# Later rotary products and weight preparation, an earlier first norm, and rebalanced helpers in a one-core decoder step

## The chip, the core and the metric

The kernel runs on one NeuronCore of a Trainium2 chip. The metric is device time in microseconds (us) of one execution. TensorE (PE in the profile) does the matrix products, VectorE (DVE), ScalarE (ACT) and GpSimd (POOL) do everything else, and all DMAs are issued from SyncE's queue (SP).

## What is computed

One layer of a hybrid decoder, for 1024 prompt positions and 8 x 4 sample positions that share the weights: 1056 columns in all, held feature-major (features on the 128 partitions, positions along the free axis). Cut to what matters here:

```python
h   = rmsnorm(x)
q, k, v, g, su, sv, xq, gates = split(h @ w_in)
A   = retention(rope(q), rope(k), v)      # 4 heads, chunks of 128, then GroupNorm and silu(g)
B   = gelu(su) * (tril(W_s) @ layernorm(gelu(sv)) + b)   # per chunk of 128, 4 channel groups
C   = cross_attention(xq, memory)         # 4 heads, 256 memory tokens
x   = x + (sig(gA)*A@w_br_ret + sig(gB)*B@w_br_sg + sig(gC)*C@w_br_x) @ w_o
z   = rmsnorm(x) @ w_up                   # then causal depthwise conv of width 3
x   = x + (gelu(conv(z)[:F]) * conv(z)[F:]) @ w_down
y   = rmsnorm(x)
```

rope turns the halves of a head: `x1*cos - x2*sin` and `x2*cos + x1*sin`.

## The kernel before

**Products.** Every float32 operand is split into a high part in the matmul's reduced type (`hi = cast(x)`, on ACT) and a low part (`lo = x - hi`, on POOL or DVE), and a product is three matmuls: high x high, high x low, low x high. A projection `fm(key, ops)` runs eight steps, one for each 128 input features; a step is nine matmuls (three terms by three column chunks of 384, 384 and 288). `psv` gives its PSUM tile `mp`, of which there are two. Small products (norm sums, retention, attention) use `ap`, also two.

**Weights.** `w_prep` takes the next weight slab (128x1024) from its DMA, casts it (`wh`, ACT) and subtracts (`wl`). The subtraction is on POOL, except for the keys in the list `LO_DVE`, for which it is on DVE. `w_ahead` calls `w_prep` when fewer than three slabs are live; `fm` calls it at two of its steps, before the step's `hook`. So a slab is prepared some two projections before it is used.

**What sets the order.** The order of instructions on each engine is that of the Python code; there is no scheduler behind it. `hook`, called after each step, (1) counts down the list that `later(n, fn)` fills and runs what is due, (2) runs one entry of `side`, and (3) advances the generator at the head of `gens` by `rate[0]` steps on average. The generators carry the work that runs beside the projections: `xnorm` (the first norm), `retention` of the head before, `sgu`, `xattn`, `half_norm`, `last_conv`, `fin`.

**The places that the change touches.**

- Head 0: q and k are projected together (`fm2`, 16 steps), then two g units of 8 steps. `xnorm` yields `YA` times, squares the last four of the eight x tiles (`xr`, ACT), adds them up (DVE), yields `YB` = 3 times, casts the sum (`rsh`, `rsl`), multiplies it with ones on PE (`ap`), and forms the reciprocal root by a table and a Newton step. The V projection of head 0 waits for the PSUM of g, which is scaled by that root.
- `rope_evac`, after each q and k: the product with the cosines from PSUM (DVE), four copies of the swapped halves (`sw`, ACT), the product with the sines (`sw`, POOL), and later the sum (DVE). Reads of one PSUM tile by two engines are ordered as the code has them.
- `retention`: for each chunk, `norm_rows` takes statistics (DVE) and gets the reciprocal root `grs` from two tiny POOL instructions; then DVE scales the row, and C multiplies into `ort`, which frees an `ap`.
- `sgu`: eight rounds of four matmuls into an `ap`, an addition from PSUM (`sgt`) and a product (`su`) on DVE.
- `xattn(h)`: `QS` splits the head's query (`xqh` ACT, `xql` DVE), `KS` a half of the cached keys.
- `gate(key)`: after a projection, DVE scales (`th`), ACT takes the tanh, and a DMA stores it.
- w_o: two halves of 528 columns, eight units each; a unit's result is added to the residual (`x2c`, DVE), squared (ACT) and summed (DVE), while `half_norm` works on the first half.
- w_down: eleven pairs of weight rows; a pair is eight units of 18 matmuls, each added into `x` by DVE. `last_conv`, in five steps, runs the last convolution's taps (`c`, DVE) beside the first units.
- The end: the last two pairs in three column ranges (512, 288, 256); `fin(c)` makes the final norm of a finished range: the sum of squares `ssf` is split (`sy`), summed by PE, and eight products `y` follow on POOL. `fin_last` is the same for the last range, with nothing behind it.

Of the kernel before, what the change touches and what calls it, by code (L numbers as in the profile page):

```python
# [9 lines left out]
F32R = mybir.dt.float32r  # L10
AF = mybir.ActivationFunctionType
ALU = mybir.AluOpType
# [62 lines left out]
HA, HB = 248, 280  # L75

LO_DVE = [k for i, k in enumerate(SLABS) if k[0] in ("km", "vm") and i % 2] + [("sv", 0, 0), ("sv", 0, 1)]


@with_exitstack  # L80
def step_kernel(ctx: ExitStack, tc: tile.TileContext, xT, memT, wslab, cst, ident_d, rope, vec, sgc, sgm, sgs,
                sret, kc, vc, hist, yT, sretp, cstate, ckT, cv, srets, sgv):
    nc = tc.nc
# [8 lines left out]
    def slot(name, dt=F32, shape=None):  # L92
        return sp.tile(shape or [P, T], dt, tag="S", name=name, bufs=NSLOT)
# [13 lines left out]
    def mm(out, l, r, start=True, stop=True):  # L107
        nc.tensor.matmul(out=out, lhsT=l, rhs=r, start=start, stop=stop)  # L108
# [4 lines left out]
    def vtt(out, a, b, op):  # L113
        nc.vector.tensor_tensor(out=out, in0=a, in1=b, op=op)  # L114

    def ptt(out, a, b, op):
        nc.gpsimd.tensor_tensor(out=out, in0=a, in1=b, op=op)  # L117
# [4 lines left out]
    def f(t):  # L122
        return t.bitcast(F32) if t.dtype == F32R else t

    def psv(ps):
        return [ps[:, 0:2, 0:384], ps[:, 2, 0:288]]

    def seg(t):
        return [t[:, 0:768].rearrange("p (a b) -> p a b", a=2), t[:, 768:1056]]
# [58 lines left out]
    def later(n, fn):  # L188
        wait.append([n, fn])
# [41 lines left out]
    def fm(key, ops, kbase=0, free=True):  # L231
        hi, lo = w_get(key)
        hv = hi.rearrange("p (k c) -> p k c", c=P)
        lv = lo.rearrange("p (k c) -> p k c", c=P)
        ps = mp()
        n = len(ops)
        for k in range(n):
            rh, rl = ops[k]
            for i, (a, r) in enumerate(((hv, rh), (hv, rl), (lv, rh))):
                for c, (c0, w) in enumerate(CH):  # L240
                    mm(ps[:, c, 0:w], a[:, kbase + k, :], r[:, c0:c0 + w],
                       start=(k == 0 and i == 0), stop=(k == n - 1 and i == 2))
            if k == 0 or k == 3:
                w_ahead()
            hook()
        if free:
            w_free(key)
        return ps
# [107 lines left out]
    with tc.manual_schedule():  # L356
# [70 lines left out]
        nc.vector.tensor_scalar(out=vecs[:, VBG:VBG + 32], in0=vecs[:, VBG:VBG + 32], scalar1=0.5, scalar2=None,  # L427
                                op0=ALU.mult)

        YA, YB = 14, 3  # L430

        def xnorm():
            for _ in range(YA):
# [41 lines left out]
        def rope_evac(ps, name):  # L475
            sw = slot("sw")
            out = slot(name)
            for o, i, c in zip(seg(out), psv(ps), seg(cosT)):
                vtt(o, i, c, ALU.mult)
            for (a, b) in ((0, 64), (64, 0)):  # L480
                for o, i in zip(seg(sw), psv(ps)):
                    nc.scalar.copy(out=o[a:a + 64], in_=i[b:b + 64])
            ptt(sw, sw, sinT, ALU.mult)
            later(4, lambda: vtt(out, out, sw, ALU.add))
            return out

        def silu_evac(ps):
# [457 lines left out]
        def xattn(h):  # L945
# [133 lines left out]

            for fn, *a in ((XA, 0), (YA, 0), (XA, 1), (YA, 1), (XB, 0), (VS, 0), (XB, 1), (XC, 0), (VS, 1), (XA, 2), (YB,),  # L1080
                           (XC, 1), (XB, 2), (XA, 3), (YC, 0), (XC, 2), (KS, h + 1, 0), (XB, 3), (YC, 1),
                           (KS, h + 1, 1), (XC, 3), (QS, h + 1), (YD,)):
                while defer:
                    defer.pop(0)()
                fn(*a)
                if fn not in (VS, KS, QS):
                    yield
# [168 lines left out]
        def gate(key):  # L1256
            ps = fm(key, hops)
            t = slot("th")
            scaled(t, ps)
            return lambda: gate_out(t, key)  # L1260
# [38 lines left out]
        for m in range(8):  # L1299
            if m == 6:  # L1300
                side.extend([g_load] * 8)
            if m == 7:
                side.extend([lambda k=k: g_scale(k) for k in range(8)])
            gate(("gb", m))()
        drain()
        rate[0] = 0.0
        side.extend([lambda: f_dma(NG), lambda: G0s(0), both(G0s, 1), lambda: f_prep0(NG), both(G0s, 3), both(G0s, 5),
# [532 lines left out]
        pctx.close()  # L1840
        mpp = pctx.enter_context(tc.tile_pool(name="mpp2", bufs=2, space=bass.MemoryType.PSUM))
        gens.append(last_conv())
        rate[0] = 1.0

        def dn_get(g):
            ws = []
# [42 lines left out]

        ssf = slot("ssf")  # L1890
        rsy = slot("rsy")
        sy3 = slot("sy3", F32R)
        FCH = ((0, 512), (512, 288), (800, 256))

        def fin(c):
            c0, w = FCH[c]
            r = rsy[:, c0:c0 + w]
            yield
            yield from rstd_cols(ssf[:, c0:c0 + w], w, r, sy3, fine=True)
            for m in range(0, 8, 2):  # L1900
                y = slot("y", shape=[P, 2, 512])
                for i in range(2):
                    ptt(y[:, i, 0:w], x2t[m + i][:, c0:c0 + w], r, ALU.mult)
                later(2, lambda m=m, y=y: dma(yT[m:m + 2, :, c0:c0 + w].rearrange("m p t -> p m t"), y[:, :, 0:w]))
                yield

        def fin_last(sqs):

            c0, w = FCH[2]
            r = rsy[:, c0:c0 + w]  # L1910
            a = ap()[:, 0:w]
            mm(a, ones, sy3[:, 0:w], stop=False)
            mm(a, ones, sy3[:, w:2 * w], start=False, stop=False)
            for i in range(2):
                mm(a, f(ones), sqs[i], start=False, stop=(i == 1))
            t = slot("rn")
            rstd_sum(a, r, t[:, 0:w])
            x = lambda m: x2t[m][:, c0:c0 + w]
            g = lambda m: vecs[:, VFN + m:VFN + m + 1]
            for m in (3, 7):  # L1920
                act(x(m), x(m), scale=g(m))
            newton(r, t[:, 0:w], t[:, w:2 * w])
            for m in range(0, 8, 2):
                y = slot("y", shape=[P, 2, 512])
                for i in range(2):
                    if m + i in (3, 7):
                        ptt(y[:, i, 0:w], x(m + i), r, ALU.mult)
                    else:
                        stt(y[:, i, 0:w], x(m + i), g(m + i), r, ALU.mult, ALU.mult)
                dma(yT[m:m + 2, :, c0:c0 + w].rearrange("m p t -> p m t"), y[:, :, 0:w])  # L1930
# [5 lines left out]
        def fin_evac(c, us, pss):  # L1936
            c0, w = FCH[c]
            sl = slice(c0, c0 + w)
            sqs = {}
            for m in us:  # L1940
                vtt(x2t[m][:, sl], x2t[m][:, sl], pss[m], ALU.add)
            for m in us:
                sqs[m] = ssf[:, sl] if m == 0 else slot("sq")[:, 0:w]
                act(sqs[m], x2t[m][:, sl], AF.Square)
            for m in us:
                if c == 2 and m > 5:
                    last_sq.append(sqs[m])
                elif m:
                    vtt(ssf[:, sl], ssf[:, sl], sqs[m], ALU.add)
            if c == 2 and us[-1] == 5:  # L1950
                nc.scalar.copy(out=sy3[:, 0:w], in_=ssf[:, sl])
                vtt(sy3[:, w:2 * w], ssf[:, sl], f(sy3[:, 0:w]), ALU.subtract)
            for m in us:
                if c < 2:
                    act(x2t[m][:, sl], x2t[m][:, sl], scale=vecs[:, VFN + m:VFN + m + 1])
# [174 lines left out]
```

## Time and profile before

| | |
|---|---|
| time, median of 3 runs (lowest to highest) | 1917.12 us (1916.0 to 1917.32) |
| the profiled execution's time | 1916.06 us |
| its span from first to last instruction | 1913.9 us |
| mean granted TensorE clock | 0.991 |
| PE busy | 1854.7 us (97%) |
| DVE, POOL, ACT busy | 1144.7, 921.5, 651.8 us |
| HBM read, written | 154.34 MB, 48.41 MB |

PE is busy for nearly the whole span, so a change is worth what it takes from, or adds to, the 59 us in which PE does nothing and the time in which its clock is low. Times in the rows are us from the span's start: a row of the timeline gives start, duration, engine, line, operation, tiles (output <- inputs), count, and in brackets the idle time of the engine just before it with what ended it.

### The profile page before, as it was taken

To read this page: it belongs to the slowest core of one execution; us is meant where nothing else is said; L and a number is where in the kernel's file an instruction comes from. 1 tells how busy PE (TensorE), PEld (TensorE's weight loads), DVE (VectorE), ACT (ScalarE), POOL (GpSimd) and SP (SyncE) were. 2 spreads that over 40 slices of the span, in tenths; PEclk is the share of its full clock that TensorE was granted. 3 is DMA by queue.
4 is the path that set the end of the run, shared out by engine and by line. 5 is a ranking of instruction groups with operands and counts; after the bars stand their busy time and mean duration, and the time that the engine had idled before them with its cause. 6 is when DMAs were issued, how large, how long until landed. Compare 5 with 4: busy or idle time off the path is not lost.

```text
span 1913.9 us, 32100 instructions
## 1 busy us (share of the span) xinstructions
PE 1854.7 (97%) x13369; PEld 1828.0 (96%) x13369; DVE 1144.7 (60%) x1610; ACT 651.8 (34%) x1016; POOL 921.5 (48%) x583
## 2 busy tenths in 40 slices
PE   8899999999999999999999999899999999999997
PEld 8899999999999998999999999899999999999996
DVE  6554545442464479332352267999999999744447
ACT  6333232421233434323211233544344344321204
POOL 2243434221643421555544533577777777754404
PEclk9999999999999999999999999999999999999998
DMA  5112131324133341426632532022222223732202
GB/s 189 54 45 93 44 105 36 132 66 156 56 135 112 124 181 55 135 90 255 241 124 79 189 140 84 34 90 79 68 90 79 67 90 120 252 133 90 76 1 91
DMA packets 59808, 204.82 MB, mean 107 GB/s; under 512 B 6608, under 2 KB 9840, under 8 KB 59664
## 3 DMA queue, kind: packets, MB, share of 16 engines
q1 hardware_dynamic: 59664, 202.78, 30.8%
q8 instruction: 105, 1.72, 0.4%
q14 instruction: 39, 0.32, 0.1%
HBM read 154.34 MB, written 48.41 MB: 106 GB/s over the span
## 4 chain that ended last, share of the span: by engine, by line
PE 50%; DVE 7%; issue 1%; ACT 1%; POOL 1%; DMA 1%; DVEq 0%; SPq 0%; POOLq 0%; ACTq 0%
PE bp L108 25%; PE mp L108 25%; DVE c L120 1%; DVE xl L114 1%; DVE x2c L120 1%; DVE fs L114 1%; DVE ssf L114 0%; DMA opr<-scr 0%; POOL opl L117 0%; DMA wr<-in_wslab 0%; DVE x L114 0%; ACT xh L1153 0%; DVE hx L114 0%; POOL acl L117 0%; POOL wls L117 0%
## 5 line engine op out<-in xcount | busy, mean ns | idle before, releaser
L117 POOL TENSOR_TENSOR wl<-wr,wh 128x1024 fp32r<-128x1024 f32 x107 | 282.7, 2645 | 438.3 <-ACT wh L152 294.7
L108 PE MATMUL bp<-xh,wh 128*128 128x264 f32 (+1 forms) x1376 | 279.2, 284 | 6.8 <-DVE th L114 2.4
L108 PE MATMUL bp<-xh,wl 128*128 128x264 f32 (+1 forms) x1376 | 280.3, 285 | 1.2 <-POOL wl L117 0.7
L108 PE MATMUL bp<-xl,wh 128*128 128x264 f32 (+1 forms) x1376 | 279.8, 285 | 0.0
L108 PEld LDWEIGHTS bp<-xh,wh 128*128 128x128 f32 x1376 | 215.0, 189 | 8.2 <-issue 3.1
L108 PEld LDWEIGHTS bp<-xh,wl 128*128 128x128 f32 x1376 | 215.0, 189 | 1.8 <-POOL wl L117 1.2
L108 PEld LDWEIGHTS bp<-xl,wh 128*128 128x128 f32 x1376 | 214.5, 189 | 0.0
L108 PE MATMUL mp<-hh,wh 128*128 128x384 f32 (+1 forms) x816 | 190.0, 340 | 4.9 <-ACT hh L111 4.8
L108 PE MATMUL mp<-hl,wh 128*128 128x384 f32 (+1 forms) x816 | 179.6, 327 | 0.3 <-DVE hl L120 0.3
L114 DVE TENSOR_TENSOR x<-x,mp 128x288 f32<-128x288 f32 (+3 forms) x167 | 105.7, 676 | 120.6 <-PE mp L108 120.6
L108 PE MATMUL mp<-hh,wl 128*128 128x384 f32 (+1 forms) x816 | 177.6, 324 | 0.0
L117 POOL TENSOR_TENSOR wl<-fs,wh 128x1024 fp32r<-128x1024 f32 x52 | 146.2, 2814 | 50.9 <-ACT wh L1179 50.4
L108 PEld LDWEIGHTS mp<-hh,wh 128*128 128x128 f32 x816 | 136.0, 191 | 7.8 <-ACT hh L111 5.4
L108 PEld LDWEIGHTS mp<-hl,wh 128*128 128x128 f32 x816 | 136.6, 190 | 1.1 <-DVE hl L120 1.0
L108 PEld LDWEIGHTS mp<-hh,wl 128*128 128x128 f32 x816 | 137.0, 189 | 0.0
L108 PE MATMUL mp<-ach,whs 128*128 128x384 f32 (+3 forms) x524 | 124.3, 326 | 4.0 <-DVE x L114 3.1
L120 DVE SCALAR_TENSOR_TENSOR c<-z,hist,c 128x1024 f32<-128x1024 f32 x88 | 125.0, 1420 | 4.3 <-ACT c L111 4.2
L108 PE MATMUL mp<-ach,wls 128*128 128x384 f32 (+3 forms) x524 | 123.7, 325 | 0.0
L108 PE MATMUL mp<-acl,whs 128*128 128x384 f32 (+3 forms) x524 | 123.4, 325 | 0.0
L152 ACT CAST wh<-wr 128x1024 fp32r<-128x1024 f32 x86 | 89.4, 1043 | 95.8 <-PE mp L108 54.2
L1179 ACT CAST wh<-fs 128x1024 fp32r<-128x1024 f32 x55 | 57.7, 1050 | 155.6 <-DVE fs L114 145.3
L120 DVE SCALAR_TENSOR_TENSOR c<-zs,hist,c 128x32 f32<-128x32 f32 x88 | 110.6, 1256 | 0.0
(367 smaller groups left out, 4161.5 us busy)
## 6 DMA issues: line engine op xcount, KB each, us to landing
wr<-in_wslab SPq DMA_DIRECT2D x162, 512.0 KB, 3.7
sg<-th SPq DMA_DIRECT2D x24, 528.0 KB, 5.2
th<-sg SPq DMA_DIRECT2D x24, 528.0 KB, 5.5
sca<-c SPq DMA_DIRECT2D x22, 528.0 KB, 3.0
opr<-sca SPq DMA_DIRECT2D x22, 528.0 KB, 4.7
opr<-scr SPq DMA_DIRECT2D x16, 528.0 KB, 7.0
scr<-ort SPq DMA_DIRECT2D x8, 528.0 KB, 7.6
hx<-in_xT SPq DMA_DIRECT2D x8, 528.0 KB, 5.9
```

Of the source, the lines that this page charges most:

```text
L108: nc.tensor.matmul(out=out, lhsT=l, rhs=r, start=start, stop=stop)
L114: nc.vector.tensor_tensor(out=out, in0=a, in1=b, op=op)
L117: nc.gpsimd.tensor_tensor(out=out, in0=a, in1=b, op=op)
L120: nc.vector.scalar_tensor_tensor(out=out, in0=a, scalar=s, in1=b, op0=op0, op1=op1)
L152: nc.scalar.copy(out=hi, in_=raw)
L1179: nc.scalar.copy(out=hi, in_=src)
```

## The change

It has nine parts.

1. `LO_DVE` gains the second half's eight w_o slabs and the slabs of xq 2 and 3.
2. `fm` calls `w_ahead` at steps 1 and 4 and not at 0 and 3.
3. `YA` is 11 and not 14.
4. `rope_evac`, head 0: the copies come ahead of the product with the cosines. Heads 1 to 3: the product with the sines is put off by two hooks, the sum from four to five.
5. `xattn`: `QS` of the next head stands two places earlier, ahead of `KS(h + 1, 1)`.
6. The tanh of the eight gb gates is put off by two hooks.
7. `rate[0]` is 0.5 and not 1.0 in the down stage, where only `last_conv` runs.
8. The final norm of the second column range starts two hooks later; four of the first range's eight `y` products are on DVE.
9. Last range: the squares of rows 3 to 5 join those of 6 and 7 as separate matmuls, and the sum split for PE (now in a tile of its own, `sy4`) holds rows 0 to 2 alone.

```diff
+LO_DVE += [("wo", m, 1) for m in range(8)]
+LO_DVE += [("xq", 2), ("xq", 3)]
...
-            if k == 0 or k == 3:
+            if k == 1 or k == 4:
                 w_ahead()
             hook()
...
-        YA, YB = 14, 3
+        YA, YB = 11, 3
...
+            def turn():
+                for (a, b) in ((0, 64), (64, 0)):
+                    for o, i in zip(seg(sw), psv(ps)):
+                        nc.scalar.copy(out=o[a:a + 64], in_=i[b:b + 64])
+            if h == 0:
+                turn()
             for o, i, c in zip(seg(out), psv(ps), seg(cosT)):
                 vtt(o, i, c, ALU.mult)
...
-            ptt(sw, sw, sinT, ALU.mult)
-            later(4, lambda: vtt(out, out, sw, ALU.add))
+            if h:
+                turn()
+            if h:
+                later(2, lambda: ptt(sw, sw, sinT, ALU.mult))
+            else:
+                ptt(sw, sw, sinT, ALU.mult)
+            later(5 if h else 4, lambda: vtt(out, out, sw, ALU.add))
...
-                           (KS, h + 1, 1), (XC, 3), (QS, h + 1), (YD,)):
+                           (QS, h + 1), (KS, h + 1, 1), (XC, 3), (YD,)):
...
-            gate(("gb", m))()
+            later(2, gate(("gb", m)))
...
-        rate[0] = 1.0
+        rate[0] = 0.5
...
-        sy3 = slot("sy3", F32R)
+        sy3, sy4 = slot("sy3", F32R), slot("sy4", F32R)
...
-            yield
+            for _ in range(3 if c else 1):
+                yield
             yield from rstd_cols(ssf[:, c0:c0 + w], w, r, sy3, fine=True)
...
-                    ptt(y[:, i, 0:w], x2t[m + i][:, c0:c0 + w], r, ALU.mult)
+                    (vtt if c == 0 and m < 4 else ptt)(y[:, i, 0:w], x2t[m + i][:, c0:c0 + w], r, ALU.mult)
...
-            for i in range(2):
-                mm(a, f(ones), sqs[i], start=False, stop=(i == 1))
+            for i in range(len(sqs)):
+                mm(a, f(ones), sqs[i], start=False, stop=(i == len(sqs) - 1))
...
-                if c == 2 and m > 5:
+                if c == 2 and m > 2:
                     last_sq.append(sqs[m])
...
-            if c == 2 and us[-1] == 5:
+            if c == 2 and us[-1] == 2:
```

POOL, head 2, around its k projection, before (`grs` belongs to the retention of head 1, `sw_2116` and `wl_2136` to k and to the next slab):

```order
L117 TENSOR_TENSOR grs_2096<-mv_2095,cB_112 128x1
L117 TENSOR_TENSOR grs_2096<-grs_2096,nhalf_78 128x1
L117 TENSOR_TENSOR sw_2116<-sw_2116,sinT_111 128x1056
L117 TENSOR_TENSOR wl_2136<-wr_1844,wh_2135 128x1024
L117 TENSOR_TENSOR grs_2153<-mv_2152,cB_112 128x1
L117 TENSOR_TENSOR grs_2153<-grs_2153,nhalf_78 128x1
```

and the same place after:

```order
L119 TENSOR_TENSOR grs_2096<-mv_2095,cB_112 128x1
L119 TENSOR_TENSOR grs_2096<-grs_2096,nhalf_78 128x1
L119 TENSOR_TENSOR grs_2146<-mv_2145,cB_112 128x1
L119 TENSOR_TENSOR grs_2146<-grs_2146,nhalf_78 128x1
L119 TENSOR_TENSOR wl_2162<-wr_1864,wh_2161 128x1024
L119 TENSOR_TENSOR sw_2116<-sw_2116,sinT_111 128x1056
```

The second pair of `grs` has moved ahead of both long instructions, which have changed places. In heads 1 and 3 only the two long ones change places there, and that pair stays behind them.

DVE, start of the spatial gating, before:

```order
L886 TENSOR_SCALAR sgS_4449<-sgS_4449,lmv_4454,lrs_4455 32x512
L114 TENSOR_TENSOR sgt_5143<-ap_5138,sgC_4447 128x512
L114 TENSOR_TENSOR su_3711<-su_3711,sgt_5143 128x512
L114 TENSOR_TENSOR sgt_5160<-ap_5155,sgC_4447 128x512
L114 TENSOR_TENSOR su_3948<-su_3948,sgt_5160 128x512
```

and after:

```order
L897 TENSOR_SCALAR sgS_4449<-sgS_4449,lmv_4454,lrs_4455 32x512
L116 TENSOR_TENSOR wl_5108<-wr_4751,wh_5107 128x1024
L116 TENSOR_TENSOR sgt_5137<-ap_5132,sgC_4447 128x512
L116 TENSOR_TENSOR su_3711<-su_3711,sgt_5137 128x512
L116 TENSOR_TENSOR wl_5150<-wr_4874,wh_5149 128x1024
L116 TENSOR_TENSOR sgt_5160<-ap_5155,sgC_4447 128x512
L116 TENSOR_TENSOR su_3948<-su_3948,sgt_5160 128x512
```

Two weight subtractions have come to DVE among the gating's rounds; on POOL they are gone from there.

DVE, head 0, from q to the norm's sum (`xr_89` is the running sum of squares, `rsl` its low part for PE), before:

```order
L114 TENSOR_TENSOR q_326<-mp_200,cosT_110 128x768
L114 TENSOR_TENSOR q_326<-mp_200,cosT_110 128x288
L114 TENSOR_TENSOR xr_87<-xr_87,xr_86 128x1056
L114 TENSOR_TENSOR k_371<-mp_201,cosT_110 128x768
L114 TENSOR_TENSOR k_371<-mp_201,cosT_110 128x288
L114 TENSOR_TENSOR q_326<-q_326,sw_325 128x1056
L114 TENSOR_TENSOR xr_89<-xr_89,xr_88 128x1056
L114 TENSOR_TENSOR xr_89<-xr_89,xr_87 128x1056
L114 TENSOR_TENSOR xr_89<-xr_89,xr_85 128x1056
L114 TENSOR_TENSOR k_371<-k_371,sw_370 128x1056
L114 TENSOR_TENSOR rsl_448<-xr_89,rsh_447 128x1056
```

and after:

```order
L116 TENSOR_TENSOR xr_87<-xr_87,xr_86 128x1056
L116 TENSOR_TENSOR q_329<-mp_200,cosT_110 128x768
L116 TENSOR_TENSOR q_329<-mp_200,cosT_110 128x288
L116 TENSOR_TENSOR xr_89<-xr_89,xr_88 128x1056
L116 TENSOR_TENSOR xr_89<-xr_89,xr_87 128x1056
L116 TENSOR_TENSOR xr_89<-xr_89,xr_85 128x1056
L116 TENSOR_TENSOR k_376<-mp_201,cosT_110 128x768
L116 TENSOR_TENSOR k_376<-mp_201,cosT_110 128x288
L116 TENSOR_TENSOR q_329<-q_329,sw_328 128x1056
L116 TENSOR_TENSOR rsl_420<-xr_89,rsh_419 128x1056
L116 TENSOR_TENSOR k_376<-k_376,sw_375 128x1056
```

The three additions of `xr_89` now stand ahead of k's product and of q's sum, and `rsl` ahead of k's sum. On ACT the squares that feed them stand ahead of the copies of k.

More of the change, by code (lines that the diff above doesn't have):

```diff
@@ L477, in rope_evac @@
             out = slot(name)
+            def turn():
[4 more added lines that the diff above has]
+                turn()
             for o, i, c in zip(seg(out), psv(ps), seg(cosT)):
                 vtt(o, i, c, ALU.mult)
-            for (a, b) in ((0, 64), (64, 0)):
-                for o, i in zip(seg(sw), psv(ps)):
-                    nc.scalar.copy(out=o[a:a + 64], in_=i[b:b + 64])
-            ptt(sw, sw, sinT, ALU.mult)
-            later(4, lambda: vtt(out, out, sw, ALU.add))
+            if h:
[5 more added lines that the diff above has]
+            later(5 if h else 4, lambda: vtt(out, out, sw, ALU.add))
             return out
@@ L1911, in fin_last @@
             a = ap()[:, 0:w]
-            mm(a, ones, sy3[:, 0:w], stop=False)
-            mm(a, ones, sy3[:, w:2 * w], start=False, stop=False)
-            for i in range(2):
-                mm(a, f(ones), sqs[i], start=False, stop=(i == 1))
+            mm(a, ones, sy4[:, 0:w], stop=False)
+            mm(a, ones, sy4[:, w:2 * w], start=False, stop=False)
+            for i in range(len(sqs)):
+                mm(a, f(ones), sqs[i], start=False, stop=(i == len(sqs) - 1))
             t = slot("rn")
@@ L1949, in fin_evac @@
                     vtt(ssf[:, sl], ssf[:, sl], sqs[m], ALU.add)
-            if c == 2 and us[-1] == 5:
-                nc.scalar.copy(out=sy3[:, 0:w], in_=ssf[:, sl])
-                vtt(sy3[:, w:2 * w], ssf[:, sl], f(sy3[:, 0:w]), ALU.subtract)
+            if c == 2 and us[-1] == 2:
+                nc.scalar.copy(out=sy4[:, 0:w], in_=ssf[:, sl])
+                vtt(sy4[:, w:2 * w], ssf[:, sl], f(sy4[:, 0:w]), ALU.subtract)
             for m in us:
```

## The prediction, made before the changed kernel had run

> **What bounds the kernel now.** I read the page's busy shares first.
>
> ```profile
> span 1913.9 us, 32100 instructions
> PE 1854.7 (97%) x13369; PEld 1828.0 (96%) x13369; DVE 1144.7 (60%) x1610; ACT 651.8 (34%) x1016; POOL 921.5 (48%) x583
> ```
>
> PE sets the end. The change leaves its products as they are but for three small sums at the end, so it acts through the 59 us (1913.9 - 1854.7) in which PE stands. The list of PE's waits, longest total first, says who ended them (total, times, longest).
>
> ```profile
> PE ap L108 <- ACT rsh L337: 5.9, 1, 5.9
> PE ap L108 <- DVE ort L120: 3.7, 3, 2.9
> PE mp L108 <- DVE x L114: 3.1, 2, 2.6
> PE ap L108 <- DVE sgt L114: 3.0, 1, 3.0
> PE mp L108 <- DVE x2c L120: 2.7, 2, 2.0
> PE ap L108 <- DVE xql L114: 2.1, 1, 2.1
> PE ap L108 <- ACT sy L319: 1.9, 1, 1.9
> ```
>
> Each belongs to a place that the change touches. A wait of two or three us costs more than itself. The table by stretches shows the granted clock (PEclk, third number from the right) after six such waits:
>
> ```profile
> 40.00:60.00 20.00, 13.51 (x71) 12.84 (x71) 10.73 (x10) 10.52 (x13) 9.73 (x19) 0.83 0.31 104
> 226.40:229.80 3.40, 2.94 (x11) 2.80 (x12) 2.74 (x5) 0.47 (x1) 0.00 (x0) 0.50 0.35 142
> 530.20:533.60 3.40, 3.18 (x13) 3.18 (x14) 3.18 (x6) 0.00 (x0) 0.00 (x0) 0.51 0.89 294
> 1156.00:1158.20 2.20, 2.20 (x12) 2.20 (x11) 2.20 (x1) 0.46 (x1) 2.02 (x1) 0.50 0.00 0
> 1656.60:1660.00 3.40, 3.03 (x10) 3.06 (x11) 3.40 (x4) 1.25 (x2) 3.40 (x2) 0.51 0.25 59
> 1892.10:1895.50 3.40, 3.28 (x15) 3.29 (x16) 3.15 (x7) 1.47 (x4) 2.44 (x2) 0.50 0.42 158
> ```
>
> The clock is half for about 3.4 us, so PE loses half of what it was busy there: 1.5 us after the `ort` and `x` waits, 1.6 after `sgt` and `sy`, 1.7 for `x2c` (a whole 3.4 us busy). A wait that shrinks well below 2 us takes this loss with it.
>
> The Trainium skill ("TensorE: Matmul & The Clock Gate", section "HAM oscillation — how this bites in real kernels") asks only for no PE gaps over about 3.4 us. By that rule gaps of 2 to 3 us would cost no clock; the rows above disagree, all six stretches but the first following a gap of at most 3 us.
>
> **The change part by part.** Gains are taken against the profiled execution (1916.06 us, 2.2 outside its span), and the same gain is then taken from the median, 1917.12, which is 1.06 above it.
>
> *First norm* (squares three steps sooner).
>
> ```profile
> 42.06 0.64 PE L108 MATMUL mp<-hh,wh 128*128 128x384 f32 x3
> 44.48 0.65 PE L108 MATMUL mp<-hh,wl 128*128 128x384 f32 x3
> 51.01 0.69 PE L108 MATMUL ap<-rsh,ones 128*128 128x384 f32 x1 [5.88 <-ACT rsh L337]
> 52.31 0.69 PE L108 MATMUL ap<-rsl,ones 128*128 128x384 f32 x1 [0.61 <-DVE rsl L114]
> 67.57 0.39 PE L108 MATMUL mp<-wh,hh 128*128 128x256 f32 x1 [1.53 <-DVE silu L114]
> 42.25 2.06 ACT L111 ACTIVATE xr<-xr 128x1056 f32<-128x1056 f32 x2
> 129.34 1.05 ACT L152 CAST wh<-wr 128x1024 fp32r<-128x1024 f32 x1
> 34.22 2.42 POOL L117 TENSOR_TENSOR wl<-wr,wh 128x1024 fp32r<-128x1024 f32 x1
> 34.79 2.96 DVE L114 TENSOR_TENSOR xr<-xr 128x1056 f32<-128x1056 f32 x1 [5.35 <-ACT xr L111]
> 44.34 5.52 DVE L114 TENSOR_TENSOR xr<-xr 128x1056 f32<-128x1056 f32 x3 [4.19 <-ACT xr L111]
> ```
>
> At stake are 5.88 + 0.61 + 1.53 of waiting and 1.7 of clock (0.17 of 20 us at half, half of it busy) = 9.7. Groups of three matmuls start 0.484 us apart (42.06 to 44.48 is five groups) and a step is three groups, 1.45 us, so PE reaches the sum three steps before 45.13 (44.48 + 0.65), at 40.8. The last squares, which ended at 44.3 (42.25 + 2.06) behind q's and k's copies, now stand behind q's alone: q's matmuls end twelve steps before 45.13, at 27.7, and copies about as long as the squares, a slab's cast of 1.05 and the squares bring it to some 33. Then three additions: 1.2 each alone, but an addition beside a POOL instruction ends only after it (34.79 ran 2.96, until 1.1 after POOL's 34.22 + 2.42). POOL has a preparation and k's sine product there, some 2.4 each. If it gets in ahead of each addition, the sum is done at 43, `rsh` a microsecond later, and `rsl`, now behind k's product and q's sum, at 46.8: PE stands 5.3 and loses 1.0 of clock. The cast for V, moved behind the roots, can also put 1.7 on Newton's step. Gain 9.7 - 8.0 = 1.7. If POOL never gets in, PE stands 2.0: gain 7.7. I take 2.5, near the low end, since both POOL instructions are ready in time; range 0 to 7.7.
>
> *Heads.*
>
> ```profile
> 218.23 0.18 DVE L525 BATCH_NORM_AGGREGATE mv<-bst 128x2 f32<-128x6 f32 x1
> 219.90 2.47 POOL L117 TENSOR_TENSOR sw<-sw,sinT 128x1056 f32<-128x1056 f32 x1 [4.66 <-ACT sw L482]
> 222.31 2.39 POOL L117 TENSOR_TENSOR wl<-wr,wh 128x1024 fp32r<-128x1024 f32 x1
> 226.86 1.62 PE L108 MATMUL ap<-V,rt 128*128 128x256 f32 x6 [2.94 <-DVE ort L120]
> ```
>
> In head 2 the statistics were ready at 218.4, but POOL came to `grs` at 224.7, after the sine product and the slab's low part. Now `grs` stands first: 2.94 + 1.5 of clock go, and I put 0.5 back for k's later sum, which now delays the next state update. In heads 1 and 3 the preparation goes first, must wait for its cast (1.05), and `grs` still follows both: their waits, (3.7 - 2.9) / 2 = 0.4 each, grow by 1.05. Sum 3.9 - 2.1 = 1.8; range 0 to 3.9.
>
> *Spatial gating* and *query split*.
>
> ```profile
> 523.79 5.98 DVE L114 TENSOR_TENSOR su<-su,sgt 128x512 f32<-128x512 f32 x1
> 524.54 4.67 POOL L117 TENSOR_TENSOR wl<-wr,wh 128x1024 fp32r<-128x1024 f32 x2
> 728.33 1.23 DVE L114 TENSOR_TENSOR wl<-fs,wh 128x1024 fp32r<-128x1024 f32 x1 [1.17 <-ACT wh L1179]
> 590.79 2.55 DVE L114 TENSOR_TENSOR xql<-xq,xqh 128x1056 fp32r<-128x1056 f32 x1 [3.15 <-ACT xqh L293]
> ```
>
> DVE's product waited through two POOL preparations until 529.8. They go to DVE at 1.23 each (728.33, the same shape there), one in each of two gating rounds: 3.0 + 1.6 of clock go and 0.5 comes back. I take 4.0 (2 to 4.5). The query split stood behind tanh and a weight cast on ACT and a preparation on POOL; earlier, it meets neither: 2.0 of the 2.1 (0 to 2.1). The later tanh also clears ACT for the other attention steps; I take 0.8 (-1 to 2), for the softmax waits are small and new collisions can come.
>
> *w_o, second half*: 3.0 in all.
>
> ```profile
> 1122.27 2.45 DVE L114 TENSOR_TENSOR ns<-ssq,ns 128x528 fp32r<-128x528 f32 x1 [0.76 <-ACT ns L1476]
> 1124.77 0.64 PE L108 MATMUL ap<-ns,ones 128*128 128x264 f32 x3 [1.67 <-DVE ns L114]
> ```
>
> The norm's split (528 columns, 2.45 us) waited out POOL's preparation; with the subtraction on DVE its 1.67 falls to about 0.55. For the `x2c` waits (2.7, with 1.7 of clock) DVE is spared three blocks of some 2 us, but gets three subtractions of 1.23 and 1 to 1.7 of waiting for a cast; I find waits of 0.6, 1.5 and 0.4, too short for the slow clock. Gain 1.1 + 4.4 - 2.5 = 3.0, range 0 to 6.
>
> *Down stage*.
>
> ```profile
> 1653.17 2.42 DVE L120 SCALAR_TENSOR_TENSOR c<-zs,hist,c 128x32 f32<-128x32 f32 x1
> 1655.52 1.30 DVE L114 TENSOR_TENSOR x<-x,mp 128x768 f32<-128x768 f32 x2
> ```
>
> With a tap after every unit DVE falls behind PE; with one after every second unit it has two units of 2.9 us (18 matmuls, two steps) for two evictions of 1.3 and a tap of at most 4.8 (two instructions, both blocked as the 2.42 is). At stake are 3.1 + 1.5 of clock; I leave 1.5 of waiting: gain 3.1 (1 to 4.6). The last convolution's store is needed eight pairs later.
>
> *End*.
>
> ```profile
> 1883.01 1.18 DVE L114 TENSOR_TENSOR x<-x,mp 128x288 f32<-128x288 f32 x3
> 1883.26 11.28 POOL L117 TENSOR_TENSOR y<-x,rsy 128x512 f32<-128x512 f32 x8 [68.59 <-DVE rsy L120]
> 1903.55 1.13 PE L108 MATMUL ap<-sq,ones 128*128 128x256 f32 x4 [0.44 <-ACT sq L111]
> ```
>
> The second range's sum moves behind two more units, so its waits (1.9 + 0.6) and 1.6 of clock go: 4.1. Against that, two `y` products now stand ahead of the eviction at 1883.01, with POOL starting its own at the same moment: 0.7 if they run through, 3.4 if POOL (11.28 / 8 = 1.4 each) gets in before both. Three more sums cost 1.6 of PE (half of 1.13 each), 1.0 of it hidden behind the last eviction. 4.1 less 2.0, the middle of these, and 0.6 is 1.5 (-2 to 4).
>
> Sum: 2.5 + 1.8 + 4.0 + 2.0 + 0.8 + 3.0 + 3.1 + 1.5 = 18.7. Every preparation in the projections shifts by a step, so I keep 2.7 for collisions not found: 16, from 1917.1 to 1901.1.
>
> **The rivals.**
>
> *Moving subtractions to DVE does not help.* Each costs DVE 1.23 and a wait for its cast, where POOL's cost DVE its block only on collision. Gating and w_o would give nothing: 16 - 7.0, about 1908. For it: DVE is the late engine in both. Against: in the gating DVE lost 5.3 us to 4.67 us of POOL. Chance 0.14. The Trainium skill ("Perfetto Trace Analysis", section "Optimizing Scalar/DVE Operations") says that offloading between these two might not help, as they share a port; the 5.98 row agrees that they exclude each other.
>
> *The end turns round.* POOL gets in before both `y`, PE stands over 3 us and its clock falls: -2 for 1.5, about 1904.6; chance 0.12.
>
> *Slower: weights arrive late.* 58 projections prepare one step (1.46) later. If each waited 0.35 us for a low part, +20 would outweigh 16: about 1921. It decides from 0.28 a projection. Against: a slab is prepared two projections ahead, so at least one of eight steps, 11.7 us, is left, and no wait for `wl` is among the long ones. Chance 0.03.
>
> *The waits re-form elsewhere*, within 3 us of no change, 1917: the low ends of the eight terms add up to zero. Chance 0.05.
>
> *Short gaps cost no clock.* Then 8 of the 18.7 are not there: 1909. The rows at half clock speak against it: 0.02. This is what the clock page's rule would give.
>
> **How the numbers follow.** The forecast has 0.62, and a gain beyond 24 (first norm and w_o at their upper ends) 0.02. Faster is 0.62 + 0.14 + 0.12 + 0.02 + 0.02 = 0.92, same 0.05, slower 0.03; 0.2%, 3.8 us, is about what a measurement tells from no change. The range 1893 to 1911 (gains of 24 and 6) holds the forecast with its bounds and the three rivals in between.
>
> **What would show it.** After: no `sgt`, `xql` or 2.9 us `ort` wait; `x` waits below 2 us in the down stage; fewer stretches at half clock (six now, one of them double); `ort` waits of 1.4 us in heads 1 and 3; a smaller `rsh`/`rsl` wait near 41 to 47. The prediction is wrong if PE's busy time with clock loss stays and idle time stays near 59 us, or if waits for `wl` appear.

## The result and the profile after

The changed kernel takes 1897.84 us (median of 4 runs, 1897.31 to 1899.15) against 1916.56 us of the kernel before (1915.51 to 1917.32) on the same chip: 18.7 us less, ratio 0.9904 with a 95% interval of 0.9887 to 0.9921. The prediction said 1901.1, from 1893 to 1911, and faster.

The head of the page of the profiled execution (1897.9 us):

```profile
span 1896.1 us, 32100 instructions
PE 1847.1 (97%) x13375; PEld 1822.9 (96%) x13375; DVE 1138.1 (60%) x1621; ACT 652.0 (34%) x1016; POOL 905.7 (48%) x569
```

The span is 17.8 us shorter. PE was busy for 7.6 us less (1854.7 to 1847.1), though it has six matmuls more. Most of that is clock: inside the stretches at half clock PE was busy for 23.2 us before and for 11.6 after, and half of the difference is 5.8. It stood for 10.2 us less (59.2 to 49.0). The list of PE's waits (total, times, longest) answers to the one of before:

```profile
PE mp L110 <- DVE x L116: 5.9, 4, 2.1
...
PE ap L110 <- ACT rsh L339: 3.2, 1, 3.2
PE ap L110 <- DVE ort L122: 2.9, 2, 1.5
...
PE ap L110 <- DVE rsl L116: 1.8, 1, 1.8
PE mp L110 <- DVE x2c L122: 1.3, 2, 0.9
...
PE ap L110 <- DVE sgt L116: 0.2, 1, 0.2
...
PE ap L110 <- ACT sy L321: 0.2, 1, 0.2
```

`xql` is gone from the list and `sgt`, `x2c`, `sy` and `ns` (1.7 to 0.5) have shrunk. `x`, which was to shrink, has grown from 3.1 to 5.9. The stretches that are still at half clock, and the four places where one stood before and none does now (the clock is the third number from the right):

```profile
40.00:60.00 20.00, 13.89 (x72) 12.97 (x71) 15.30 (x12) 6.24 (x7) 7.91 (x9) 0.83 0.19 55
223.00:227.00 4.00, 4.00 (x27) 3.70 (x26) 3.38 (x4) 0.47 (x1) 3.41 (x2) 1.00 0.42 131
524.00:528.00 4.00, 3.88 (x29) 3.88 (x30) 3.68 (x7) 1.05 (x1) 0.54 (x1) 1.00 0.83 276
1136.00:1140.00 4.00, 3.49 (x29) 3.52 (x30) 3.05 (x5) 1.63 (x3) 0.00 (x0) 1.00 0.22 84
1211.40:1214.80 3.40, 3.40 (x18) 3.40 (x17) 3.37 (x6) 1.34 (x5) 1.29 (x1) 0.50 0.64 214
1648.30:1651.70 3.40, 3.40 (x13) 3.40 (x12) 2.54 (x3) 0.83 (x1) 3.40 (x2) 0.50 0.01 5
1874.00:1878.00 4.00, 3.73 (x30) 3.62 (x30) 3.02 (x9) 3.12 (x9) 0.00 (x0) 1.00 0.91 338
```

The first norm and the down stage still have theirs, and the stretch in the up stage (1211) stood in the profile before too, near 1230. So there were seven, the first of them double, and there are three. Head 2, the gating, w_o and the end have lost theirs.

From V's first matmul to the last sums PE executes the same products in the same order, so the start of one matmul in both traces gives the lead at that place:

| the matmul | before | after | lead, us |
|---|---|---|---|
| V's first, after the first norm | 67.57 | 66.40 | 1.2 |
| `sgW` product ahead of the gating's wait | 525.08 | 521.50 | 3.6 |
| `hl` product behind it | 533.18 | 525.60 | 7.6 |
| `xqh` / `xql` product | 590.81 / 593.40 | 582.65 / 582.88 | 8.2 / 10.5 |
| last long softmax wait | 703.25 | 688.78 | 14.5 |
| w_o, ahead of the norm | 1031.12 | 1016.39 | 14.7 |
| w_o, behind its half clock | 1158.02 | 1139.26 | 18.8 |
| ahead of the down stage | 1565.82 | 1547.26 | 18.6 |
| down stage, behind its half clock | 1669.37 | 1651.74 | 17.6 |
| last matmul | 1904.30 | 1884.79 | 19.5 |
| end of the span | 1913.9 | 1896.1 | 17.8 |

Leads of half a us at the start mean nothing: the run with the ten subtractions alone (below), whose first norm is that of before, is 0.5 us late at V's first matmul.

### The profile page after: what moved, and what is told of

It reads as the page before. It is cut to its first block, busy times and chain, and to the rows that moved or that the text cites. A ratio compares the mean times of both kernels' runs of the same rounds, so it can differ in the third digit from the quotient of the medians.

```text
span 1896.1 us, 32100 instructions
## 1 busy us (share of the span) xinstructions
PE 1847.1 (97%) x13375; PEld 1822.9 (96%) x13375; DVE 1138.1 (60%) x1621; ACT 652.0 (34%) x1016; POOL 905.7 (48%) x569
## 4 chain that ended last, share of the span: by engine, by line
PE 51%; DVE 7%; ACT 1%; issue 1%; POOL 1%; DVEq 0%; ACTq 0%
PE bp L110 26%; PE mp L110 25%; DVE c L122 2%; DVE xl L116 1%; DVE x2c L122 1%; DVE fs L116 0%; DVE wl L116 0%; ACT sq L113 0%; DVE hx L116 0%; DVE x L116 0%; POOL opl L119 0%; DVE z L116 0%; ACT xh L1164 0%; DVE ssf L116 0%; DVE c L116 0%
## 5 line engine op out<-in xcount | busy, mean ns | idle before, releaser
L119 POOL TENSOR_TENSOR wl<-wr,wh 128x1024 fp32r<-128x1024 f32 x97 | 258.5, 2666 | 424.7 <-ACT wh L154 285.0
```

## The experiments

Where an edit has several parts, they lie far apart in time and each is read at its place, by the same comparison of starts. Ratios are to the kernel before; the changed kernel's is 0.9904.

### The ten subtractions back on POOL

```diff
-LO_DVE += [("wo", m, 1) for m in range(8)]
-LO_DVE += [("xq", 2), ("xq", 3)]
```

> The changed kernel with the ten low-part subtractions (w_o second half, xq 2 and 3) back on POOL. Theory (POOL's 2.4 us preparation stops DVE's two-operand work; on DVE it costs 1.23): the gating's sgt wait comes back near 3 us with its half clock, 3 to 4.5 us there; in w_o the ns wait returns from 0.53 to about 1.7 and the x2c waits grow by 1 to 2 with 1.7 of clock, 2.5 to 4.5 us there. In all 1897.8 to about 1903.5 to 1907. Rival (the preparation one step later had cleared both places, the engine does not matter): under 1 us at each place, 1897 to 1899.

Measured: 1906.24 us, ratio 0.9944 (0.9928 to 0.9961). The timeline of PE has all three waits back:

```profile
526.38 1.16 PE L108 MATMUL ap<-sgW,vg 128*128 128x128 f32 x8 [2.98 <-DVE sgt L114]
1113.70 0.63 PE L108 MATMUL ap<-ns,ones 128*128 128x264 f32 x3 [1.67 <-DVE ns L114]
1142.73 0.72 PE L108 MATMUL mp<-mg,wh 128*128 128x264 f32 x4 [1.97 <-DVE x2c L120]
```

The gating loses 4 us with its half clock and w_o 2.9, here without a half clock. The engine of the subtraction matters at both places; the later preparation alone had cleared neither.

### The ten subtractions alone

The kernel before with those two lines added.

> The kernel before with the ten subtractions on DVE and nothing else. Theory (the part works by itself): the gating's sgt wait falls from 2.96 to under 0.5 and its half clock goes, 3.5 to 4.5 us; the ns wait from 1.67 to 0.55 and the x2c waits to about 1.5 with no half clock, 3.5 to 4.5 us; in all 1907.5 to 1910. Rival (it needs the later preparation): sgt or x2c waits of 2 us stay, under 4 us gained in all, 1913 to 1917.

Measured: 1911.96 us, ratio 0.9969 (0.9958 to 0.998): 5.1 us faster than before, between the two expectations. w_o gains its 4.0 us, in full and alone. In the gating the long wait is gone, but one of 0.94 stands in its place, so 3.3 come. The `xql` wait stays, and this time has a half-clock stretch behind it, which costs 1.5; in head 2, where nothing was edited, the stretch lasts twice as long as before and costs 1.1:

```profile
591.82 0.58 PE L110 MATMUL ap<-mmh,xql 128*128 128x256 f32 x1 [2.08 <-DVE xql L116]
```

### The preparation's step: undone, and alone

Undone, from the changed kernel:

```diff
-            if k == 1 or k == 4:
+            if k == 0 or k == 3:
                 w_ahead()
```

> The changed kernel with the weights prepared at steps 0 and 3 of a projection again. Theory (the engines' shares and the order in the heads carry the gain, the step itself little): heads 1 and 3 keep their 1.45 us ort waits, because POOL's order there stays as it is; in head 2 the preparation now stands ahead of grs, but the sine product does not, so its wait stays below 0.5 us; the attention loses 0 to 2 us by collisions on ACT. In all 1898 to 1900. Rival (the step is what cleared the attention's 4 us): 1901 to 1903, with pt, xt and y waits back between 600 and 705. No wait for wl of half a us or more that was not there, by either.

Measured: 1907.65 us, ratio 0.9952 (0.9937 to 0.9967). Both expectations missed: the gating loses 0.7 and the attention gains 1.7, and the heads lose 9.7 us, 7.3 of them in head 2. Its timeline (POOL, DVE, PE):

```profile
224.77 0.55 POOL L119 TENSOR_TENSOR grs<-grs,nhalf 128x1 f32<-128x1 f32 x1
225.28 2.41 POOL L119 TENSOR_TENSOR sw<-sw,sinT 128x1056 f32<-128x1056 f32 x1
225.35 2.49 DVE L541 TENSOR_SCALAR cB<-cB,mv,grs 128x256 f32<-128x256 f32 x1 [5.76 <-POOL grs L119]
228.77 1.62 PE L110 MATMUL ap<-V,rt 128*128 128x256 f32 x6 [3.96 <-DVE ort L122]
```

`grs` is late, behind the slab. And when it is done, POOL goes on at once with the sine product, 0.07 us before DVE can start the scaling that waited for `grs`. The scaling took 0.42 before; here it takes 2.49, to the end of POOL's instruction. In the changed kernel the two do not meet:

```profile
219.10 0.55 POOL L119 TENSOR_TENSOR grs<-grs,nhalf 128x1 f32<-128x1 f32 x1
221.59 2.40 POOL L119 TENSOR_TENSOR wl<-wr,wh 128x1024 fp32r<-128x1024 f32 x1 [1.95 <-ACT wh L154]
223.95 2.46 POOL L119 TENSOR_TENSOR sw<-sw,sinT 128x1056 f32<-128x1056 f32 x1
```

What stands right behind `grs` is the slab, which still waits for its cast, and DVE has 1.95 us; the scaling, at 220.66, takes 0.41.

Alone, in the kernel before, the same step moved to 1 and 4:

> The kernel before with the weights prepared at steps 1 and 4 and nothing else. Query split: theory (with the preparation a step later neither ACT's cast nor POOL's subtraction stands in front of it) the xql wait of 2.08 falls below 0.7, some 1.5 to 2 us gained; rival (the split's place or the tanh is needed) it stays near 2. Heads: grs is ahead of the preparation but behind the sine product, so head 2 keeps an ort wait of 2.5 to 3 us as in v_sin and nothing is gained there. Gating: sgt wait near 3 as before, 0. In all by the theory 1914 to 1916.5, by the rival 1917.

Measured: 1913.4 us (10 runs), ratio 0.9984 (0.9975 to 0.9994), 2.7 us faster. The `xql` wait is gone and so is the `pt` wait of 0.93, 3.8 us between 590 and 720 (2.0 at the query split, 1.8 behind it), though one of 1.2 for `ox` has come there. On ACT `xqh` now stands ahead of the slab's cast, so `xql` takes 1.26 where it took 2.55 through POOL's subtraction. Head 2 keeps its wait (below) and the heads lose 2.5 in all, with new waits of 0.65 to 0.71. The gating's 2.96 stays, and so does the `rsh` wait of 5.9 in the first norm. Some 2 us of this trace's gain are clock that the edit does not explain: the waits for `x2c` in w_o (1.99) and for `x` in the down stage (2.59) are those of before, but have no half clock behind them.

```profile
228.76 0.95 PE L108 MATMUL ap<-V,rt 128*128 128x256 f32 x6 [2.71 <-DVE ort L120]
```

So this part by itself clears the query split and brings 1.8 of the 4.0 us that the change gains in the rest of the attention. With the others in place, undoing it brings none of that back: there more than one part suffices.

### The sine product at once again

```diff
-                later(2, lambda: ptt(sw, sw, sinT, ALU.mult))
+                ptt(sw, sw, sinT, ALU.mult)
...
-            later(5 if h else 4, lambda: vtt(out, out, sw, ALU.add))
+            later(4, lambda: vtt(out, out, sw, ALU.add))
```

> The changed kernel with the product with the sines at once again in heads 1 to 3 (sum after four hooks); the preparation stays a step later. Theory (the two parts only work together: grs must be ahead of both POOL instructions, and whatever starts right behind grs stops DVE's scaling of the row for 2.4 us): head 2 has an ort wait of 2.5 to 4 us again with half clock, heads 1 and 3 keep 0.4 to 1.5; 3 to 7 us slower, 1901 to 1905. Rival (the preparation's step is what clears head 2): ort wait below 1 us in head 2, 1897 to 1899.

Measured: 1902.76 us, ratio 0.9922 (0.9905 to 0.9938). Head 2's wait is back, without a half clock:

```profile
228.32 0.96 PE L110 MATMUL ap<-V,rt 128*128 128x256 f32 x6 [2.69 <-DVE ort L122]
```

Behind `grs` POOL starts the slab at 224.88, and the scaling, 0.07 us later, takes 2.44.

Heads 1 and 3 gain a us each (ort waits of 0.38 and 0.34 instead of 1.46 and 1.44), and lose it to waits of 0.67 to 0.95 for `st` and `ort` elsewhere. The heads' gain needs both parts, the later slab and the later product: either alone is worse than the kernel before (2.5 us with the step alone, some 7 in the run above that has the product's delay and not the step).

### YA, the tanh and the down stage's rate undone

```diff
-        YA, YB = 11, 3
+        YA, YB = 14, 3
...
-            later(2, gate(("gb", m)))
+            gate(("gb", m))()
...
-        rate[0] = 0.5
+        rate[0] = 1.0
```

> The changed kernel with three parts undone that lie far apart and are read each at its place: YA 14 again, the gb tanh at once, and one tap after each unit in the down stage. Theory: the first norm loses 1 to 2 us (rsh wait 5.9 instead of 3.2 + 1.8, the same 6.8 us at half clock); the attention loses 2 to 3.5 us (pt waits of 0.3 to 0.9 come back, since the tanh stands ahead of the casts of pt on ACT); the down stage gains 0.5 to 1.5 us (waits of 3.1 instead of 3.8, one half-clock stretch in both). In all 1899.5 to 1902. Rival for the attention (the tanh's place does nothing, the preparation's step or DVE's subtraction cleared it): 0 to 0.5 us there and 1898. Rival for the down stage (rate 0.5 helps): it loses 1 to 3 us there.

Measured: 1895.86 us, ratio 0.9889 (0.9874 to 0.9904): not slower, but 2 us faster than the changed kernel. The first norm is 2.4 us faster without the "squares three steps sooner". First the changed kernel's timeline (DVE, POOL, PE), then this one's:

```profile
33.42 9.77 DVE L116 TENSOR_TENSOR xr<-xr 128x1056 f32<-128x1056 f32 x3 [1.72 <-ACT xr L113]
32.86 2.41 POOL L119 TENSOR_TENSOR wl<-wr,wh 128x1024 fp32r<-128x1024 f32 x1
35.68 3.04 POOL L119 TENSOR_TENSOR sw<-sw,sinT 128x1056 f32<-128x1056 f32 x1 [0.41 <-ACT sw L483]
38.69 3.38 POOL L119 TENSOR_TENSOR wl<-wr,wh 128x1024 fp32r<-128x1024 f32 x1
44.35 0.69 PE L110 MATMUL ap<-rsh,ones 128*128 128x384 f32 x1 [3.15 <-ACT rsh L339]
46.81 0.69 PE L110 MATMUL ap<-rsl,ones 128*128 128x384 f32 x1 [1.77 <-DVE rsl L116]
```

```profile
40.25 6.04 DVE L116 TENSOR_TENSOR xr<-xr 128x1056 f32<-128x1056 f32 x3
47.45 0.44 PE L110 MATMUL ap<-rsh,ones 128*128 128x384 f32 x1 [1.42 <-ACT rsh L339]
48.74 0.44 PE L110 MATMUL ap<-rsl,ones 128*128 128x384 f32 x1 [0.85 <-DVE rsl L116]
64.04 0.38 PE L110 MATMUL mp<-wh,hh 128*128 128x256 f32 x1 [1.53 <-DVE silu L116]
```

With YA 11 three additions meet three POOL instructions, each ends after one of them, and three take 9.77 us where an undisturbed one takes 1.24. PE reaches the sum 4.8 us sooner (at 41.2 instead of 46.0), but the sum itself comes only 3.1 sooner. PE's waits there are 6.1 us in the changed kernel, with one of 1.18 ahead of the root's transposes for which the profile names no cause, and 3.8 with YA 14. The Trainium skill ("SBUF — State Buffer", section "SBUF: two separate sides") says that DVE with two SBUF inputs and GpSimd take a pair of ports as an exclusive lock for a whole instruction; the 9.77 agrees.

The tanh at once costs the attention 1.2 us, between the expectations. The down stage is 1.5 faster with the rate of 1.0: waits of 0.52 and 2.56 in place of 1.75 and 2.06, and no half clock behind them. The kernel before has the same rate, almost the same waits (0.52 and 2.59) and a half clock, so by the waits only 0.7 of it belongs to the rate.

### Head 0's copies, and three parts of the attention together

```diff
-            if h == 0:
-                turn()
             for o, i, c in zip(seg(out), psv(ps), seg(cosT)):
                 vtt(o, i, c, ALU.mult)
-            if h:
-                turn()
+            turn()
```

and, in the attention, the tanh at once, `QS` two places later and xq 2 and 3 off `LO_DVE`.

> The changed kernel with head 0's copies behind the product with the cosines again (YA stays 11), and, far from it, the three parts undone together that touch the attention (tanh at once, query split late, xq subtractions on POOL). First norm: theory (the copies ahead are what brought the squares forward, YA 11 itself costs) 2 to 4 us slower there, rsh wait above 5 us; rival (YA does it) 0 to 0.5. Attention: theory (each part alone suffices, since tanh or split or subtraction undone alone cost 1.2, 0 and 0 there) with all three undone the xql wait of 2 us comes back and pt and y waits with it, 3 to 6 us; rival (none matters, something else cleared it) about 1.2, the tanh's own. The gating loses its 3.7 us as with the subtractions on POOL. In all 1904 to 1910 by the theories, 1902 to 1903 by the rivals.

Measured: 1905.62 us, ratio 0.9936 (0.9922 to 0.9951). The first norm is 1.8 us slower, with a `rsh` wait of 5.18. The leads of V's first matmul in all twelve traces go by the combination of YA and copies: copies late and YA 14, 0 to -0.5 us (three traces); copies late and YA 11, -0.6 (this one); copies early and YA 11, -0.1 to 1.6 (five); copies early and YA 14, 3.5 to 5.6 (three). The gain of the first norm belongs to the copies, not to YA. In the attention the three undone cost 2.8 us, 1.2 of them the tanh's (a wait of 1.23 for `ox` stands in both runs); the `xql` wait does not come back, since the preparation's step alone clears it (above). The gating loses its 4 us again.

### The query split and the products y undone

```diff
-                           (QS, h + 1), (KS, h + 1, 1), (XC, 3), (YD,)):
+                           (KS, h + 1, 1), (XC, 3), (QS, h + 1), (YD,)):
...
-                    (vtt if c == 0 and m < 4 else ptt)(y[:, i, 0:w], x2t[m + i][:, c0:c0 + w], r, ALU.mult)
+                    ptt(y[:, i, 0:w], x2t[m + i][:, c0:c0 + w], r, ALU.mult)
```

> The changed kernel with the query split two places later again, and all eight y of the first column range on POOL. Theory: the xql wait before the first key product returns only if POOL and ACT still collide with it: 1 to 2.4 us; at the end the eviction is no longer behind two y on DVE, so the x wait of 1.39 us at 1869 goes, but POOL is busy for 11 us instead of 6.4 and stops the sums of squares, which gives 0.5 to 1 back: a gain of 0.4 to 1 there. In all 1898 to 1899.5. Rival for the end (y on DVE is what lets the sums through): 1 to 2 us slower there, sy waits above 1 us.

Measured: 1899.6 us, ratio 0.9911 (0.9896 to 0.9925). The place of `QS` does nothing (no start moves by more than 0.3 between 200 and 1200). At the end the rival is right: 1.3 us slower. The changed kernel's end, then this one's:

```profile
1865.48 2.40 DVE L116 TENSOR_TENSOR y<-x,rsy 128x512 f32<-128x512 f32 x2
1867.80 1.17 DVE L116 TENSOR_TENSOR x<-x,mp 128x288 f32<-128x288 f32 x3
1869.03 0.39 PE L110 MATMUL mp<-ach,whs 128*128 128x256 f32 x1 [1.39 <-DVE x L116]
```

```profile
1868.69 3.71 DVE L116 TENSOR_TENSOR ssf<-ssf,sq 128x288 f32<-128x288 f32 x3
1880.27 0.90 PE L110 MATMUL ap<-sy,ones 128*128 128x288 f32 x2 [2.81 <-ACT sy L321]
```

The `x` wait goes, but 11.3 us of POOL stretch the sums until `sy` is 2.81 late, with a half clock behind it.

### A version with four new edits

```diff
-        YA, YB = 11, 3
+        YA, YB = 14, 3
...
-            if k == 1 or k == 4:
+            if k in at:       # (1, 4); (3, 5) in g's first projection of heads 1 and 3
...
-                later(2, lambda: ptt(sw, sw, sinT, ALU.mult))
-            later(5 if h else 4, lambda: vtt(out, out, sw, ALU.add))
+                later(4 if h % 2 else 2, lambda: ptt(sw, sw, sinT, ALU.mult))
+            later((4, 6, 5, 6)[h], lambda: vtt(out, out, sw, ALU.add))
...
-            pa.tap(1)
+            pa.tap(1, 0)      # the 1024 prompt columns
             yield
+            pa.tap(1, 1)      # the 32 sample columns
+            yield
...
-                    (vtt if c == 0 and m < 4 else ptt)(
+                    (vtt if m in ((4, 6), (2, 4))[c] else ptt)(
```

> The changed kernel with four new edits, each read at its place. (1) YA 14 again: as measured with it alone, waits of 1.4 and 0.9 in place of 3.2 and 1.8, 2.4 us gained. (2) Heads 1 and 3: preparation in g's projection at steps 3 and 5, sine product after four hooks, sum after six, so that grs stands first on POOL: ort waits of 1.45 go below 0.3, 2.5 us gained. (3) Down stage: a tap's two instructions in two steps, so that no piece holds DVE for more than 3.4 us: theory (an eviction may come 3.2 us late, two buffers less one eviction's and one unit's time) x waits of 1.75 and 2.06 go below 0.4 and the half clock with them, 3 to 5 us gained; rival (DVE lacks throughput there) waits of 1 to 2 us stay, under 1.5 gained. (4) End: y of the first range on DVE for rows 4 to 7 and not 0 to 3, y of the second for rows 2 to 5: theory x wait of 1.39 us at the eviction goes and the tail after the last sum shrinks from 10.9 to about 10, 2 to 3.5 us gained; rival (sums of squares late instead, as with all y on POOL) sy wait above 1 us, nothing gained. In all 1887 to 1890 by the theories, 1892 to 1896 by the rivals.

Measured: 1886.25 us (1884.27 to 1887.15), ratio 0.9836 (0.9821 to 0.985), some 13 us below the changed kernel by the ratios. (`tap(j, part)` issues that part alone; the other three taps are split in the same way.) The first norm gains 4.4 us, its waits are those with YA 14 and early copies above, and no half clock stands behind them; that is 2 us more than expected, and with it the time is below the expected range although the fourth edit brought nothing. Heads 1 and 3 lose their `ort` waits and the small one behind, 2 us each. The down stage gains some 5.5 (3.8 of waiting, 1.7 of clock) and has neither a wait above 0.3 nor a half clock. Its DVE, first in the changed kernel with the wait that it made:

```profile
1640.78 3.35 DVE L122 SCALAR_TENSOR_TENSOR c<-z,hist,c 128x1024 f32<-128x1024 f32 x1
1644.05 2.43 DVE L122 SCALAR_TENSOR_TENSOR c<-zs,hist,c 128x32 f32<-128x32 f32 x1
1646.40 2.53 DVE L116 TENSOR_TENSOR x<-x,mp 128x768 f32<-128x768 f32 x4
1647.85 0.83 PE L110 MATMUL mp<-ach,whs 128*128 128x384 f32 x3 [2.06 <-DVE x L116]
```

and in this version:

```profile
1637.07 2.50 DVE L122 SCALAR_TENSOR_TENSOR c<-z,hist,c 128x1024 f32<-128x1024 f32 x1
1639.50 1.30 DVE L116 TENSOR_TENSOR x<-x,mp 128x768 f32<-128x768 f32 x2
```

A unit is 2.9 us, an eviction 1.3, and there are two buffers. So an eviction may start 1.6 us after its unit has ended, and a piece that starts right behind one eviction may hold DVE for 5.8 less two evictions, 3.2 us, before the next one makes PE wait. (The expectation calls these 3.2 us the lateness of the eviction itself.) In the changed kernel the first blocked tap, from 1633.49, takes 2.54 + 2.44, some 4.9, and PE waits 1.75, as 4.9 less 3.2 says; the second, above, takes 3.35 + 2.43, some 5.7, and PE waits 2.06 (less than 5.7 less 3.2, since the first wait had put its unit back). Halves of 3.4 at most stay within 0.2 of the 3.2. At the end only the place of the wait changed: 1.57 at the eviction and 1.42 for `sy`; the rival was right there.

### All y of the first range on DVE

As the version above, with `vtt if c == 0 or m in (2, 4) else ptt`, one hook later.

> As v_best, but all eight y of the first column range are on DVE, and start one hook later. Theory (POOL's y stop DVE's sums of squares and its y, 2.4 us more in each of two places; alone on DVE a pair of y takes 1.3): the sums take 1.4 instead of 3.7, the x wait of 1.57 and the sy wait of 1.42 fall below 0.5, 2 to 3 us gained, 1883 to 1884.5. Rival (DVE is short of time there whoever does the y): waits of 1 us or more stay, 1885.5 to 1887.

Measured: 1885.56 us (1885.15 to 1887.22), ratio 0.9843 (0.9828 to 0.9858): no difference to the version above. The sums take 1.58 instead of 3.73 and the `x` wait is gone, as the theory says, but the products hold the next eviction and `sy` is 2.40 late. That fits the rival, by which DVE is short of time at the end; what would cure it was not tried further.

## Why the prediction was right, and where it was not

The time lies in the range, and the sum of the terms, 18.7, is the measured gain. That is partly luck: errors of both signs cancel, and the 2.7 held back for collisions was not needed beside them.

| term | predicted (range) | measured |
|---|---|---|
| first norm | 2.5 (0 to 7.7) | 1.2 |
| heads | 1.8 (0 to 3.9) | 2.4 |
| gating | 4.0 (2 to 4.5) | 4.0 |
| query split | 2.0 (0 to 2.1) | 2.4 |
| other attention | 0.8 (-1 to 2) | 4.0 |
| w_o | 3.0 (0 to 6) | 4.0 |
| down stage | 3.1 (1 to 4.6) | -0.9 |
| end | 1.5 (-2 to 4) | 0.2 |

The measured terms are differences of the leads above; the half a us that is missing to 17.8 lies between the places.

*First norm.* The working of the sum held row by row: the sum was to be done at 43 with POOL ahead of each addition, and was at 43.2; `rsl` was to come at 46.8, and its matmul started at 46.81; PE was to stand 5.3, and stood 4.9. The clock did not follow it: its loss was to fall from 1.7 to 1.0, and went from 2.0 to 2.4 (half of 4.07 and of 4.75 us that PE was busy at half clock). In place of the 1.7 put on Newton's step, for which no row stood, there is the wait of 1.18. The step that failed is the credit: YA was given the gain. Head 0's copies made it, and YA 11 takes 2.4 of it back.

*Heads.* Right in each part: head 2's wait and half clock are gone, and heads 1 and 3 wait 1.46 and 1.44 where 0.4 + 1.05 was predicted. What it missed is that the order leaves DVE a gap behind `grs`; with the sine product or the slab there the scaling takes 2.4 to 2.5 us and not 0.4.

*Gating and w_o.* Right: taking the subtractions away from POOL is what clears them, shown in both directions. The rival that moving them to DVE does not help is wrong. In the changed kernel it costs 7.7 us by the ratios to put them back; the rival had 7.0 to lose. The block that was held against moving work between the two is there, but at the late place a subtraction takes 1.2 us on DVE and 2.4 on POOL. In w_o the `x2c` waits kept 1.3 us and not the 2.5 of the sum.

*Query split and other attention.* The effect was right, the cause not. The split's place is worth nothing, and the later preparation, for which only losses were looked for (the weights late), clears the split's wait by itself. The term for the attention was mis-sized, 0.8 against 4.0: the preparation's own gain, 1.8 alone, was not in it, and the tanh has 1.2; which parts make the rest was not separated. No new wait for a slab appeared.

*Down stage.* The failed step is "it has two units of 2.9 us for two evictions of 1.3 and a tap of at most 4.8", with 1.5 of waiting left. That is a balance of time, 7.4 against 5.8 once per tap. What counts is the one piece between two evictions, 3.2 us at most, which no rate makes shorter; the taps took 4.9 and 5.7. Two waits of 1.75 and 2.06 re-formed, the second above the 2 us that the prediction had named, with the half clock.

*End.* The eviction waits 1.39, as in the case taken; the `sy` waits fell as predicted, and at the last matmul the lead had grown by 1.9. Then 1.7 of it were lost behind the last matmul, which the sum had not priced. Of these 1.2 are in the last Newton step: the second range's `y`, two hooks later, run on POOL beside it, and its operations take 0.69, 0.90 and 0.90 where they took 0.41, 0.43 and 0.42.

*Short gaps cost no clock.* Wrong, as expected; 5.8 of the 17.8 us are clock, against 8 in the sum. The stretches before were counted as six; the seventh, in the up stage, was overlooked, and the change leaves it.

## What to carry to other kernels

A queue's next instruction matters as much as the one waited for: what stands right behind a small one that another engine waits for can block the engine that it has just released (0.42 us became 2.49 here), unless it has to wait itself. A buffer's slack is a delay and not a rate: take the longest piece that can stand between two evictions, and cut it below the slack. Where several parts of a change meet at one place, undoing one says only whether it is needed, and doing one alone whether it suffices; here the two answers differ for the attention and for the heads.

## What the hardware showed unexpectedly

Whether a wait of some 2 us costs clock changes from trace to trace. In the run with YA, the tanh and the rate undone and in the version with four edits the first norm has the same waits, 1.42, 0.85 and 1.53 against these:

```profile
46.95 0.44 PE L110 MATMUL ap<-rsh,ones 128*128 128x384 f32 x1 [1.41 <-ACT rsh L339]
48.24 0.44 PE L110 MATMUL ap<-rsl,ones 128*128 128x384 f32 x1 [0.85 <-DVE rsl L116]
62.01 0.38 PE L110 MATMUL mp<-wh,hh 128*128 128x256 f32 x1 [1.53 <-DVE silu L116]
```

The stretches behind them, first of the run with three parts undone, then of the version:

```profile
49.40:52.80 3.40, 3.40 (x13) 3.40 (x12) 0.56 (x1) 1.88 (x3) 1.99 (x1) 0.50 0.00 0
```

```profile
40.00:60.00 20.00, 17.74 (x111) 17.21 (x110) 13.64 (x12) 6.24 (x7) 10.00 (x18) 1.00 0.31 106
```

From the first sum to V's first matmul the one takes 16.6 us and the other 15.1. In the up stage the same wait for `z`, 2.1 us, has a half clock behind it in the changed kernel (1211 above); with the split and `y` undone it has none, and the slow stretch stands 15 us later, behind another wait of 2.0 us:

```profile
1210.40:1214.90 4.50, 3.84 (x31) 3.84 (x32) 4.47 (x5) 2.23 (x5) 2.44 (x3) 1.00 0.41 119
1226.50:1229.90 3.40, 3.40 (x18) 3.40 (x17) 2.92 (x7) 0.48 (x1) 3.27 (x2) 0.51 0.54 167
```

The four runs of the version spread from 1882.1 to 1885.2 us of span, with mean clocks from 0.997 to 0.995: two stretches of 3.4 us at half clock are 0.002 of the mean clock and 3.4 us of time. So a part of under 2 us is judged by its waits, not by one run's time. The Trainium skill ("TensorE: Matmul & The Clock Gate", section "What's actually happening") has a window of 3413 ns that runs free of the kernel; the stretches of 3.41 us and the changes from trace to trace agree. The same section of the Trainium skill has the clock fall after an idle window of about 3.4 us; the waits of 2 to 3 us above, with a half clock behind them, do not agree with that.
